# A router's table of overflow places, kept in memory by token instead of by block

## The chip, the cores and the metric

The kernel runs on one core of a Trainium2 chip. The metric is the device time of one execution in microseconds (us); the time of a version is the median of its runs. A profile is one further execution, recorded by the hardware profiler.

## The reference

Two blocks are computed on 256 tokens of width 1024. The first block is a mixer (an RWKV part and a gated linear attention part), an output projection, and a mixture of 32 experts; the second is a two-layer transformer with a context stream of its own. The piece that matters here is the routing of the first block's experts. Cut to that:

```python
gsel = jnp.argmax(coarse, axis=-1)                       # one of 4 groups per token
top_p, top_e = lax.top_k(pf, TOP_K)                      # 2 of the 8 experts of the group
eid = (gsel[:, None] * 8 + top_e).reshape(-1)            # 512 assignments, 2 per token
counts = jnp.bincount(eid, length=32)                    # tokens of each expert
...
ys = (silu(xb @ w_gate[e]) * (xb @ w_up[e])) @ w_down[e] # block by block
out = segment_sum(ys * row_w[:, None], row_tok)          # back to the tokens, weighted
```

## The kernel before, in words

**Two tasks share the engines.** A planner (`_run`) interleaves two streams of work while the program is written: the first block (the function `first`, which ends in `moe`, tiles named with a trailing m), and the conditioning and the context stream of the second block (`second`, tiles named with a trailing c). The order of TensorE's work and of SyncE's loads is the order in which the planner wrote it and is not rearranged later; the other engines are ordered by a scheduler when the program is built.

**Weights come in pieces of 512 KB.** `raw` (line 313) issues each load on SyncE's queue (SP) into one of 13 buffers: 8 called raw, and 5 called room that exist during the context's first feed-forward layers. They are used in rings, so a raw load takes the buffer of the raw load eight before it, and a room load that of the room load five before it. A piece of `wi` or `wo` (feed-forward weights) is split into two parts before TensorE uses it: ScalarE writes `whi` (line 319), VectorE writes `wlo` (line 320), and the buffer is then free; TensorE does 24 matmuls with it (lines 334 to 336, three for each of eight 128x128 tiles). A piece of `moe_gu` (expert weights) is used by TensorE directly, in 4 matmuls (line 1338), and its buffer is free after them.

**Completion counters.** The transfers that SP and ScalarE (ACT) issue share eight completion counters, called DMAHW0 to DMAHW7, which they take in turn. An issue that takes a counter waits until the transfer that had it before has landed.

**The router.** `route` computes for each token its two experts, its rank in each, and from these its place in the blocks of 32 tokens that overflow an expert's first 32. Each expert's first 32 tokens are handled in `moe`, whose first group of four experts follows the router directly. The overflow is handled much later by a loop, `moe_over` (line 1366), which runs `nover` times, a number that the router computes and that can be zero. The loop needs the place of every token in block b: for each of 128 token rows four numbers (two experts by two halves of the tokens). The router builds them in the tile `pos`, [128, 4, 16] (tile name oposm), and writes it to the memory tensor `pos_d`, declared as [16, 128, 4]: block outermost, so that the loop reads one contiguous 2 KB block. Since `pos` has the block innermost and `pos_d` has it outermost, neighbours in `pos` lie 2 KB apart in `pos_d`. Two other transfers go out on ACT's queue near it, `tok_d` (1 MB) and `exp_d` (0.1 KB).

Of the kernel before, what the change touches and what calls it, by code (L numbers as in the profile page):

```python
# [10 lines left out]
F32 = mybir.dt.float32  # L11
# [4 lines left out]
OP = mybir.AluOpType  # L16
# [214 lines left out]
class _Net:  # L231
# [888 lines left out]
    def route(self, ch, x):  # L1120

        nc = self.nc
        mm, V, A = nc.tensor.matmul, nc.vector, nc.scalar
# [4 lines left out]
        b = ch.bank()  # L1128
# [28 lines left out]
        iota = self.c("iota")  # L1157
# [62 lines left out]
        b = ch.bank()  # L1220
# [20 lines left out]
        p = 0  # L1241
        for d in (1, 2, 4, 8, 16):
            V.tensor_copy(inc[1 - p][:, :d], inc[p][:, :d])
            V.tensor_tensor(inc[1 - p][:, d:], inc[p][:, d:], inc[p][:, :32 - d], op=OP.add)
            p = 1 - p
        inc = inc[p]
        V.tensor_tensor(t, inc, nb, op=OP.subtract)
        V.tensor_scalar(t, t, 32.0, -32.0, op0=OP.mult, op1=OP.add)
        pos = ch.tile([128, 4, 16], "opos")
        for a in range(2):  # L1250
            for i in range(2):
                g, r = ch.tile([128, 2], "og", bufs=2), ch.tile([128, 32], "ogt", bufs=2)
                V.tensor_tensor(r, rk[:, i], oh[a][:, i], op=OP.mult)
                V.reduce_sum(g[:, 0:1], r, axis=AX.X)
                V.tensor_tensor(r, t, oh[a][:, i], op=OP.mult)
                V.reduce_sum(g[:, 1:2], r, axis=AX.X)
                V.tensor_tensor(g[:, 1:2], g[:, 1:2], g[:, 0:1], op=OP.add)
                V.tensor_scalar(g[:, 0:1], g[:, 0:1], 32.0, None, op0=OP.is_ge)
                V.scalar_tensor_tensor(g[:, 1:2], g[:, 1:2], 1.0, g[:, 0:1], op0=OP.add, op1=OP.mult)
                V.tensor_scalar(pos[:, 2 * a + i], iota[:, :16], -32.0, -1.0, op0=OP.mult, op1=OP.add)  # L1260
                V.tensor_scalar(pos[:, 2 * a + i], pos[:, 2 * a + i], g[:, 1:2], None, op0=OP.add)
        nc.scalar.dma_start(self.tok_d, self.htok)
        nc.scalar.dma_start(self.pos_d.rearrange("b p a -> p a b"), pos)
        V.tensor_copy(self.cw[:, 0:2], c1)
        V.tensor_copy(self.cw[:, 2:4], c2)
        cmpt = ch.tile([128, 16, 32], "ocm")
# [99 lines left out]
    def moe_over(self, ch_of, x):  # L1366

        nc, tc = self.nc, self.tc
        mm, V, A = nc.tensor.matmul, nc.vector, nc.scalar
        n = nc.values_load(self.nover, min_val=0, max_val=15)  # L1370
        with tc.For_i(0, n, 1) as blk:
            with ExitStack() as es:
                ch = ch_of(es)
                eg = ch.tile([1, 2], "veg", I32)
                nc.sync.dma_start(eg, self.exp_d[bass.ds(blk, 1)])
                ps = ch.tile([128, 4], "vps")
                nc.sync.dma_start(ps, self.pos_d[bass.ds(blk, 1)].rearrange("b p a -> (b p) a"))
                gq = nc.sync.value_load(eg[0:1, 0:1], min_val=0, max_val=7)
                gj = nc.sync.value_load(eg[0:1, 1:2], min_val=0, max_val=3)
                eqs, sw = ch.tile([128, 2, 2, 32], "veq"), ch.tile([128, 2, 32], "vsw")  # L1380
                s = ch.tile([128, 2, 32], "vs")
                htok = ch.tile([128, 2, D], "vtok")
                nc.sync.dma_start(htok, self.tok_d)
                for i in range(2):
                    for a in range(2):
                        V.tensor_scalar(eqs[:, i, a], self.c("iota"), ps[:, 2 * a + i:2 * a + i + 1], None, op0=OP.is_equal)
                    V.tensor_tensor(s[:, i], eqs[:, i, 0], eqs[:, i, 1], op=OP.add)
                    V.tensor_scalar(sw[:, i], eqs[:, i, 0], self.cw[:, i:i + 1], None, op0=OP.mult)
                    V.scalar_tensor_tensor(sw[:, i], eqs[:, i, 1], self.cw[:, 2 + i:3 + i], sw[:, i], op0=OP.mult, op1=OP.add)
                b = ch.bank()  # L1390
                for k in range(KD):
                    for i in range(2):
                        mm(b[:, k * 32:k * 32 + 32], htok[:, i, k * 128:k * 128 + 128], s[:, i],
                           start=(i == 0), stop=(i == 1))
                xt = ch.tile([128, KD, 32], "vx")
                A.copy(xt.rearrange("p a b -> p (a b)"), b[:, :256])
                b = ch.bank()
                for i in range(2):
                    nc.tensor.transpose(b[:32, i * 128:i * 128 + 128], sw[:, i], self.ident)
                swt = ch.tile([32, T], "vwt")  # L1400
                V.tensor_copy(swt, b[:32, :T])
                gu = self.d["moe_gu"].rearrange("(g k m) p (j n) -> g m j p k n", g=8, m=2, j=4)
                dn = self.d["moe_dn"].rearrange("(g k m) p (j n) -> g m j p k n", g=8, m=2, j=4)
                bb = [ch.bank(), ch.bank()]
                for m in range(2):
                    for q in range(2):
                        r = ch.tile([128, 4, 512], "vr", bufs=2)
                        nc.sync.dma_start(r, gu[bass.ds(gq, 1), m, bass.ds(gj, 1), :, q * 4:q * 4 + 4]
                                          .rearrange("g j p k n -> (g j p) k n"))
                        for k in range(4):  # L1410
                            mm(bb[m][:32], xt[:, q * 4 + k], r[:, k], start=(q + k == 0), stop=(q == 1 and k == 3))
                ht = _all(self.swiglu_rows(ch, bb[0], bb[1], 32))
                bb = [ch.bank(), ch.bank()]
                y = ch.tile([32, 2, 512], "vy")
                for m in range(2):
                    r = ch.tile([128, 4, 512], "vr", bufs=2)
                    nc.sync.dma_start(r, dn[bass.ds(gq, 1), m, bass.ds(gj, 1)].rearrange("g j p k n -> (g j p) k n"))
                    for k in range(4):
                        mm(bb[m][:32], ht[:, k], r[:, k], start=(k == 0), stop=(k == 3))
                    A.copy(y[:, m], bb[m][:32])  # L1420
                for d in range(KD):
                    b = ch.bank()
                    mm(b[:, :T], y[:, d // 4, (d % 4) * 128:(d % 4) * 128 + 128], swt, start=True, stop=True)
                    V.tensor_tensor(x[:, d], b[:, :T], x[:, d], op=OP.add)
# [551 lines left out]
def _all(gen):  # L1976

    while True:
        try:
            next(gen)  # L1980
        except StopIteration as e:
            return e.value
# [53 lines left out]
def tile_net(ctx, tc, d, voff, coff, out):  # L2036
    nc = tc.nc
    pool = tc.tile_pool
    net = _Net(tc, d, voff[0], coff[0])
    ctx.enter_context(tc.manual_schedule(engines={mybir.EngineType.PE, mybir.EngineType.SP}))  # L2040
    base = ctx.enter_context(pool(name="base", bufs=1))
    dram = ctx.enter_context(pool(name="dram", bufs=1, space=bass.MemoryType.DRAM))
    net.scr = [dram.tile([2, 16, 4, 32, 32], F32, name=f"scr{i}") for i in range(2)]
    net.pos_d = dram.tile([16, 128, 4], F32, name="pos_d")
    net.exp_d = dram.tile([16, 2], I32, name="exp_d")
    net.tok_d = dram.tile([128, 2, D], F32, name="tok_d")
    names = ("ka", "va", "kb", "vb")
# [89 lines left out]
    with right(name="m2", bufs=1) as sb, ExitStack() as es:  # L2137
        ps = ExitStack()
        ch = _Chain("z", sb, ps.enter_context(pool(name="ps2", bufs=4, space=PSUM)), right, nw_scope=5)
# [36 lines left out]
```

## Time and profile before

| | |
|---|---|
| median of 3 runs | 2956.92 us (2956.76 to 2959.7) |
| the profiled execution's own time | 2956.47 us |
| its span on the core | 2954.7 us |
| TensorE busy | 2829.1 us, 96% of the span |
| mean granted clock of TensorE | 0.978 |
| issue of `pos_d` | at 495.68 us of the span |

The span is the stretch that the profiler sees; the execution's own time is 1.8 us longer. Times in the rows are counted from the start of the span.

### The profile page before, as it was taken

How to read it: one execution, taken by the hardware profiler on the slowest of the kernel's cores; microseconds unless marked ns; L12 is line 12 of the kernel's file. 1: busy time of each engine (PE TensorE's matmuls, PEld its weight loads, DVE VectorE, ACT ScalarE, POOL GpSimd, SP SyncE). 2: the span in 40 equal slices, each digit the busy share in tenths (PEclk: the TensorE clock that was granted, in tenths of full speed). 3: DMA queues.
4: the chain of work that ended last, by engine and by line, in shares of the span. 5: the costliest groups of instructions: out<-in, count | busy, mean ns of one | idle time of the engine just before them, and what ended most of it. 6: DMA issues, size and time to landing. Idle time of an engine off the chain costs nothing. (4 is left out here: it accounts for less than half of the span.)

```text
span 2954.7 us, 55032 instructions
## 1 busy us (share of the span) xinstructions
PE 2829.1 (96%) x22394; PEld 2391.7 (81%) x22394; DVE 1781.4 (60%) x3517; ACT 1235.9 (42%) x2071; POOL 179.2 (6%) x207
## 2 busy tenths in 40 slices
PE   8999787899999999999999899999999999999999
PEld 5656456787756778877887799889999999899999
DVE  4565564454535564555555766767766767666865
ACT  3321123333324443343333444555554545465543
POOL 0110110000000010000000000000200000101100
PEclk9999888999999999999999899999999999999999
DMA  8755856897787888797987555523455555423453
GB/s 320 252 178 173 297 214 167 296 326 265 251 275 275 309 285 326 286 366 302 350 306 286 183 195 184 189 79 116 164 193 194 184 194 197 136 92 138 169 193 131
DMA packets 198897, 667.47 MB, mean 226 GB/s; under 512 B 36850, under 2 KB 37874, under 8 KB 198002
## 3 DMA queue, kind: packets, MB, share of 16 engines
q1 hardware_dynamic: 180144, 656.04, 63.3%
q10 hardware_dynamic: 18498, 7.90, 1.3%
q8 instruction: 176, 2.88, 0.4%
q14 instruction: 79, 0.65, 0.1%
HBM read 658.05 MB, written 5.80 MB: 225 GB/s over the span
## 5 line engine op out<-in xcount | busy, mean ns | idle before, releaser
L320 DVE TENSOR_TENSOR wlo<-raw,whi 128x1024 fp32r<-128x1024 f32 x623 | 769.8, 1236 | 490.5 <-ACT whi L319 476.0
L319 ACT CAST whi<-raw 128x1024 fp32r<-128x1024 f32 x631 | 662.1, 1050 | 770.4 <-issue 274.5
L334 PE MATMUL bz<-hnhz,whi 128*128 128x256 f32 x1920 | 540.6, 282 | 0.7 <-ACT hnhz L328 0.7
L335 PE MATMUL bz<-hnlz,whi 128*128 128x256 f32 x1920 | 533.5, 278 | 4.2 <-DVE hnlz L329 4.2
L336 PE MATMUL bz<-hnhz,wlo 128*128 128x256 f32 x1920 | 532.8, 277 | 0.9 <-DVE wlo L320 0.9
L334 PE MATMUL bc<-hnhc,whi 128*128 128x256 f32 x1504 | 435.1, 289 | 15.5 <-ACT whi L319 14.7
L335 PE MATMUL bc<-hnlc,whi 128*128 128x256 f32 x1504 | 422.2, 281 | 4.5 <-DVE hnlc L469 2.9
L336 PE MATMUL bc<-hnhc,wlo 128*128 128x256 f32 x1504 | 421.9, 280 | 4.4 <-DVE wlo L320 4.4
L334 PEld LDWEIGHTS bz<-hnhz,whi 128*128 128x128 f32 x1920 | 362.1, 189 | 9.6 <-issue 5.7
L335 PEld LDWEIGHTS bz<-hnlz,whi 128*128 128x128 f32 x1920 | 362.2, 189 | 5.6 <-DVE hnlz L329 5.4
L334 PEld LDWEIGHTS bc<-hnhc,whi 128*128 128x128 f32 x1504 | 287.3, 191 | 98.1 <-issue 36.4
L336 PEld LDWEIGHTS bz<-hnhz,wlo 128*128 128x128 f32 x1920 | 362.4, 189 | 1.1 <-DVE wlo L320 1.1
L335 PEld LDWEIGHTS bc<-hnlc,whi 128*128 128x128 f32 x1504 | 287.2, 191 | 6.7 <-DVE hnlc L469 5.2
L336 PEld LDWEIGHTS bc<-hnhc,wlo 128*128 128x128 f32 x1504 | 286.5, 191 | 6.1 <-DVE wlo L320 6.1
L334 PE MATMUL bz<-h0z,whi 128*128 128x256 f32 x704 | 194.3, 276 | 0.0
L335 PE MATMUL bz<-h1z,whi 128*128 128x256 f32 x704 | 194.3, 276 | 0.0
L336 PE MATMUL bz<-h0z,wlo 128*128 128x256 f32 x704 | 194.3, 276 | 0.0
L334 PE MATMUL bc<-h0c,whi 128*128 128x256 f32 x528 | 150.4, 285 | 0.7 <-ACT h0c L328 0.7
L1338 PE MATMUL bm<-raw,mxm 128*32 128x512 f32 x752 | 147.4, 603 | 0.8 <-DMA raw<-moe_gu 0.8
L335 PE MATMUL bc<-h1c,whi 128*128 128x256 f32 x528 | 146.2, 277 | 0.9 <-DVE h1c L329 0.9
L336 PE MATMUL bc<-h0c,wlo 128*128 128x256 f32 x528 | 146.1, 277 | 0.0
L320 DVE TENSOR_TENSOR wlo<-room,whi 128x1024 fp32r<-128x1024 f32 x75 | 91.8, 1225 | 86.0 <-ACT whi L319 81.8
(702 smaller groups left out, 5319.7 us busy)
## 6 DMA issues: line engine op xcount, KB each, us to landing
raw<-wi SPq DMA_DIRECT2D x263, 512.0 KB, 4.6
raw<-moe_gu SPq DMA_DIRECT2D x188, 512.0 KB, 7.2
raw<-wada SPq DMA_DIRECT2D x144, 512.0 KB, 4.9
raw<-wo SPq DMA_DIRECT2D x124, 512.0 KB, 4.5
raw<-wbr SPq DMA_DIRECT2D x108, 512.0 KB, 3.7
raw<-win SPq DMA_DIRECT2D x104, 512.0 KB, 5.2
raw<-moe_dn SPq DMA_DIRECT2D x103, 512.0 KB, 6.0
room<-moe_gu SPq DMA_DIRECT2D x68, 512.0 KB, 9.0
```

The costliest lines, as they stand in the source:

```text
L319: self.nc.scalar.copy(hi, src)
L320: eng.tensor_tensor(lo, src, hi.bitcast(F32), op=OP.subtract)
L334: mm(out, w[0], x[0], start=first, stop=False, **kw)
L335: mm(out, w[0], x[1], start=False, stop=False, **kw)
L336: mm(out, w[1], x[0], start=False, stop=last, **kw)
L1338: mm(b[32 * j:32 * j + 32], xt[:, k, 32 * j:32 * j + 32], r[:, j % 2 * 512:j % 2 * 512 + 512], start=(k == 0), stop=(k == KD - 1))
```

## The change

The table is declared by token: [128, 16, 4] in memory, so that each of the 128 token rows has 64 numbers (256 bytes) in one piece. The tile `pos` has the same shape, [128, 16, 4], so the write of the table copies row to row. VectorE now writes each of the four columns of `pos` with a step of four numbers. The loop reads, for block b, four numbers (16 bytes) out of each token's 256 bytes, 128 pieces 256 bytes apart, where it read 128 pieces of 16 bytes that lay side by side.

```diff
@@ route
-        pos = ch.tile([128, 4, 16], "opos")
+        pos = ch.tile([128, 16, 4], "opos")
...
-                V.tensor_scalar(pos[:, 2 * a + i], iota[:, :16], -32.0, -1.0, op0=OP.mult, op1=OP.add)
-                V.tensor_scalar(pos[:, 2 * a + i], pos[:, 2 * a + i], g[:, 1:2], None, op0=OP.add)
+                V.tensor_scalar(pos[:, :, 2 * a + i], iota[:, :16], -32.0, -1.0, op0=OP.mult, op1=OP.add)
+                V.tensor_scalar(pos[:, :, 2 * a + i], pos[:, :, 2 * a + i], g[:, 1:2], None, op0=OP.add)
         nc.scalar.dma_start(self.tok_d, self.htok)
-        nc.scalar.dma_start(self.pos_d.rearrange("b p a -> p a b"), pos)
+        nc.scalar.dma_start(self.pos_d, pos)
@@ moe_over
-                nc.sync.dma_start(ps, self.pos_d[bass.ds(blk, 1)].rearrange("b p a -> (b p) a"))
+                nc.sync.dma_start(ps, self.pos_d[:, bass.ds(blk, 1)].rearrange("p b a -> p (b a)"))
@@ tile_net
-    net.pos_d = dram.tile([16, 128, 4], F32, name="pos_d")
+    net.pos_d = dram.tile([128, 16, 4], F32, name="pos_d")
```

No engine's instructions change places. On ScalarE the one row that differs is the issue of the table, between the transfer of `exp_d` and the work on the context's feed-forward layer (`wc`, `h0c`, `whi`); this is that piece of the difference, with the counters each row waits for in brackets:

```order
 L1275 DMA exp_d<-oeim 2x16x1 [waits DMAHW2_49,DVE_49]
 L1550 ACTIVATE wc<-bc 128x256 [waits PE_49,Activation_49]
-L1263 DMA pos_d<-oposm 512x16x1 [waits DMAHW4_49,DVE_49]
+L1263 DMA pos_d<-oposm 128x64 [waits DMAHW4_49,DVE_49]
 L328 CAST h0c<-wc 128x256 [waits DVE_49]
 L319 CAST whi<-room 128x1024 [waits DMAHW3_49,Activation_49]
```

The table's write has moved nowhere; it goes from 512 rows of 16 single numbers to 128 rows of 64 numbers. It takes counter DMAHW4 in both.

On SyncE nothing differs. These are its loads around the same place of the program, the same before and after (the number behind a name is the buffer's, which the later text uses to tell pieces apart):

```order
L313 DMA raw_4862<-wi0 128x1024 [waits DMAHW5_49,DMAHW1_49,DVE_49]
L313 DMA raw_4892<-wi0 128x1024 [waits DMAHW6_49,PE_49]
L313 DMA room_4931<-wi0 128x1024 [waits DMAHW7_49,PE_49]
L313 DMA raw_4961<-wi0 128x1024 [waits DMAHW0_49]
L313 DMA room_4999<-moe_gu 128x1024 [waits PE_49]
L313 DMA raw_5004<-wi0 128x1024 [waits DMAHW2_49]
L313 DMA raw_5034<-wi0 128x1024 [waits DMAHW3_49,PE_49]
L313 DMA room_5072<-moe_gu 128x1024 [waits DMAHW4_49,PE_49]
L313 DMA raw_5076<-moe_gu 128x1024 [waits DMAHW5_49]
L313 DMA room_5081<-wi0 128x1024 [waits DMAHW6_49,PE_49]
L313 DMA raw_5111<-wi0 128x1024 [waits DMAHW7_49]
L313 DMA raw_5149<-moe_gu 128x1024 [waits DMAHW0_49,PE_49]
```

The load of `room_5072` waits for counter DMAHW4, the table's, in both versions.

## Rows read from the trace of the kernel before

**Rows 1.** Page, busy time of each engine: us, share, instructions.

```profile
PE 2829.1 (96%) x22394; PEld 2391.7 (81%) x22394; DVE 1781.4 (60%) x3517; ACT 1235.9 (42%) x2071; POOL 179.2 (6%) x207
```

**Rows 2.** Busy time by stretch; columns: stretch, us, each engine, PEclk, DMA share, GB/s.

```profile
553.01:600.00 46.99, 46.99 (x388) 39.27 (x387) 25.11 (x33) 17.22 (x23) 0.00 (x0) 1.00 0.98 377
502.88:553.01 50.13, 31.63 (x205) 26.89 (x205) 14.30 (x18) 11.90 (x17) 0.00 (x0) 0.80 0.87 168
```

**Rows 3.** Waits of TensorE from 490 to 560 us: total, times, longest.

```profile
PE bc L334 <- ACT whi L319: 13.3, 3, 11.0
PE bm L1338 <- DMA room<-moe_gu: 2.7, 1, 2.7
PE bc L336 <- DVE wlo L320: 1.7, 3, 0.8
PE bm L1338 <- DMA raw<-moe_gu: 0.8, 1, 0.8
```

**Rows 4.** Timeline of TensorE, 518 to 543 us: start, length, instruction, [idle before, releaser].

```profile
518.73 0.58 PE L334 MATMUL bc<-hnhc,whi 128*128 128x256 f32 x1 [10.95 <-ACT whi L319]
...
520.58 0.41 PE L335 MATMUL bc<-hnlc,whi 128*128 128x256 f32 x1
520.80 0.41 PE L336 MATMUL bc<-hnhc,wlo 128*128 128x256 f32 x1
...
542.86 1.05 PE L1338 MATMUL bm<-room,mxm 128*32 128x512 f32 x4 [2.71 <-DMA room<-moe_gu]
```

**Rows 5.** Waits of SyncE's queue from 490 to 560 us: total, times, longest.

```profile
SPq L313 <- DMA pos_d<-oposm: 35.1, 1, 35.1
```

**Rows 6.** Timeline of SyncE's issues, 502 to 539 us.

```profile
502.49 1.25 SPq L313 DMA_DIRECT2D raw<-wi  x2
538.93 0.33 SPq L313 DMA_DIRECT2D room<-moe_gu  x1
```

**Rows 7.** The tensor `pos_d`: its issue (duration in ns, start), and time to landing.

```profile
L1263 ACTq DMA_DIRECT2D pos_d<-oposm x1: 742/742/742, 495.7 to 495.7; - x1
...
DMA to landing us min/median/max: 43.2/43.2/43.2
```

**Rows 8.** DMA from 495 to 540 us: queues with packets, MB, share; one issue group.

```profile
q1 hardware_dynamic: 1159, 4.22, 53.9%
q10 hardware_dynamic: 8208, 0.03, 26.6%
...
raw<-wi SPq DMA_DIRECT2D x5, 512.0 KB, 20.9
```

**Rows 9.** DMA over the whole span, issues by kind: KB each, median us to landing.

```profile
raw<-wi SPq DMA_DIRECT2D x263, 512.0 KB, 4.6
...
ttx<-scr ACTq DMA_DIRECT2D x2, 256.0 KB, 10.2
```

**Rows 10.** Timeline of TensorE: 24 matmuls apart; the first group's expert pieces.

```profile
494.50 0.62 PE L1338 MATMUL bm<-room,mxm 128*32 128x512 f32 x2
...
499.79 0.39 PE L334 MATMUL bc<-hnhc,whi 128*128 128x256 f32 x1
...
526.08 0.28 PE L334 MATMUL bc<-hnhc,whi 128*128 128x256 f32 x1
...
528.90 0.28 PE L334 MATMUL bc<-hnhc,whi 128*128 128x256 f32 x1
```

**Rows 11.** VectorE instructions: duration in ns min/median/max, first and last start.

```profile
L1261 DVE TENSOR_SCALAR oposm<-oposm,ogm x4: 216/217/229, 492.6 to 495.4; 128x16 f32<-128x16 f32 x4
L1436 DVE SCALAR_TENSOR_TENSOR silua<-silca,vec x2: 157/160/163, 5.0 to 5.0; 128x8 f32<-128x8 f32 x2
L1437 DVE TENSOR_SCALAR cond<-silua x2: 169/172/175, 5.2 to 5.3; 128x8 f32<-128x8 f32 x2
```

**Rows 12.** Waits of TensorE from 556 us to the end: two on weights.

```profile
PE bc L334 <- ACT whi L319: 1.4, 2, 1.0
...
PE bm L1348 <- DMA raw<-moe_dn: 0.8, 1, 0.8
```

## The prediction

> **What bounds the kernel now.** TensorE is busy 96% of the span [rows 1], so an edit counts only where TensorE stands still or runs slowly. I looked for such a place around the issue of the table, stretch by stretch. From 553.01 to 600 us TensorE is busy without a gap at clock 1.00. In the 50.13 us before that it is busy for only 31.63, at a mean clock of 0.80, and the DMA moves 168 GB/s where it moves 377 right afterwards, although its engines show 87% busy [rows 2]. So 18.50 us of standstill lie in one short stretch, beside slow running. The waits name all of it: 13.3, 2.7, 1.7 and 0.8 us, together 18.5, and every one is for weights: the first and third for a piece that is split before use, the second and fourth for an expert piece [rows 3]. The timeline shows the two large ones, 10.95 us before 518.73 and 2.71 before 542.86. It shows too what comes after the first: neighbouring matmuls start 0.22 us apart [rows 4], the lower of the clock's two levels (1.2 GHz), after eleven idle microseconds.
>
> Next, why the weights are late. SyncE, which issues them, waited once for 35.1 us, and what it waited for is the landing of `pos_d` [rows 5]. In its timeline two issues stand at 502.49, 1.25 us long, and then nothing until 538.93, a load of an expert piece into a room buffer [rows 6]; by the order of the loads that is `room_5072`, the one that takes the table's counter. The table itself was issued at 495.7 and landed 43.2 us later, at 538.9 [rows 7]. In those 45 us the queue of ScalarE carried 8208 packets with 0.03 MB: the table's 8,192 numbers, one packet each. SyncE's queue carried only 4.22 MB, and the five raw loads of `wi` in the stretch took 20.9 us to land [rows 8], against 4.6 us over the whole span [rows 9].
>
> The table thus does harm twice. The loads issued beside it crawl, which gives the wait of 10.95 us; and the loads that should follow are not issued, which gives the waits from 542.86 on.
>
> **The write.** It goes from 8,192 pieces of 4 bytes to 128 pieces of 256 bytes. No row shows a write of 256-byte pieces. From below: at the old price per piece, 43.2 us / 8,192 = 5.3 ns, 128 pieces are 0.7 us. From above: the slowest small transfer on ScalarE's queue, 256 KB, lands in 10.2 us [rows 9]. I take 4.6 us, the landing of a weight piece of sixteen times as many bytes. It then lands at 500.3, before SyncE comes to `room_5072` at 502.49 + 1.25 = 503.7, and the wait of 35.1 us is gone. At 10.2 us it lands at 505.9 and SyncE waits 2.2 us; what covers that is worked out below.
>
> **The loads.** SyncE's next condition is a free buffer. `room_5072` takes the buffer of the room load five before it and `raw_5076` that of the raw load eight before it; both held expert pieces of the first group, which TensorE has used up by 499.79 [rows 10]. The same holds for `room_5081` and `raw_5111`. So these four are issued at once, behind 503.7. After that a load needs one more piece to be split, and TensorE sets that pace.
>
> **TensorE.** At full clock the 24 matmuls of a `wi` piece take 528.90 - 526.08 = 2.82 us, and the first group's twelve expert pieces took 499.79 - 494.50 = 5.29 us, 0.44 each [rows 10]. In the 50.13 us TensorE did 205 matmuls [rows 2]: eight `wi` pieces (192) and three expert pieces (12), within one. With no wait and no slow clock these need 8 x 2.82 + 3 x 0.44 = 23.9 us, say 24.0 with the switches between the two kinds. The stretch shrinks by 50.13 - 24.0 = **26.1 us**: 18.5 of standstill and 7.6 of slow running.
>
> Are the weights there in time? Eleven pieces are 5.8 MB, over 24 us 240 GB/s, well under the 377 that the DMA gives right afterwards [rows 2]. `room_5072` is wanted after seven `wi` pieces, at 502.88 + 7 x 2.82 = 522.6. Were the table to land at 505.9 and the load to take 10.2 us as well, it would be there at about 516.5; the cover is six microseconds, and the table could land some 16 us after its issue before TensorE felt it. What may stay are the short waits for `wlo`, 1.7 us in all [rows 3]; I take nothing, since I put them down to the standstills before them, and keep 1.7 for the range.
>
> **VectorE.** Eight instructions on `pos` write with a step of 16 bytes. The second four take 217 ns each. The nearest row with a step writes 8 numbers 128 bytes apart in 172 ns, beside 160 for a write of as many side by side [rows 11]: 12 ns more for 8 numbers, 25 for 16, 0.2 us for eight instructions; from below nothing. They cost nothing as long as TensorE has its expert pieces to do, until 499.79, and 0.2 us without that cover.
>
> **The loop.** Before and after it would read 128 pieces of 16 bytes. None of its body's instructions stands in the trace: on these inputs no expert overflows and it runs zero times. The new read costs nothing here.
>
> **After 553 us.** What is won there must last to the end. From 556 us on TensorE waited 1.4 us for `whi` at line 334 and 0.8 for an expert piece [rows 12], the kinds that cost 13.3 and 3.5 in the stretch; nothing there is of the size of the gain. The order is fixed, and with buffers fuller than before at the same place of the program no load can come later. All of it stays, and at most these 2.2 us come on top.
>
> **The sum.** The profiled execution took 2956.47 us, 0.45 less than the median of the runs. 2956.47 - 26.1 = 2930.4, which I give as **2930.5**; with 1.7 us of waits kept and 2.2 won on top it runs from 2928 to 2932.5.
>
> **The rivals.** (a) *The splits become the bound.* With the loads in time, each `wi` piece still passes ScalarE and VectorE before TensorE has it. If each of the eight waited as the three for `wlo` did, 1.7 / 3 = 0.57 us [rows 3], 4.5 us would come back: 2935. For it: 13.3 us of the waits name a split. Against it: between the two standstills no wait for a split stands in the rows but those at their ends. (b) *The table lands late all the same*, because what is slow is its way into memory and not the number of its pieces. If the loads beside it run freely but it still lands at 538.9, TensorE works on until 522.6 and then stands until about 542.9, when `room_5072` lands as now. The gain falls by 20.3 us to 5.8: 2951. Against it: 8,192 packets in 43.2 us is a steady cost per packet [rows 7, 8], and weight pieces of 512 KB land in 4.6. (c) *Nothing changes*, the loads being slow for a reason of their own: 2956. Against it the wait that names the table [rows 5]. (d) *Slower, by the step in* `pos`: it decides from 26.1 / 8 = 3.3 us more for each of the eight instructions, on the way to the splits that TensorE waits for; at 4 us each it would be 2956.5 + 32 - 26 = 2962. The row with a step of 128 bytes speaks against it, with 12 ns more, not 3.3 us [rows 11].
>
> The Trainium skill has a rule on rival (d), in "SBUF — State Buffer", section "Door 1: The DMA port swizzle": the memory has lines of 16 bytes, and each access that goes on to a new line pays. With a step of four numbers every write is on a new line. The trace agrees in sign with its 12 ns and not in a size that would matter here.
>
> **How the numbers follow.** The forecast holds with 0.82. Rival (a) has 0.09, (b) 0.04, (c) 0.04, (d) 0.01. The range takes the forecast's 2928 to 2932.5 and rival (a)'s 2935, with a microsecond or two on either side for terms that add: 2926.5 to 2937, which leaves out about one in ten. Faster by over 0.2% (5.9 us, about what a measurement of this kernel can tell from no change) are the forecast, (a) and half of (b): 0.93. Within 0.2% are (c) and the rest of (b): 0.06. Slower: 0.01.
>
> **What would show it.** In the profile of the changed kernel: ScalarE's queue has some 8,000 packets fewer; `pos_d` lands in under 11 us; SyncE's wait for it is gone, with issues going on past 503.7; the `wi` loads beside it land in about 5 us instead of 20.9; TensorE is busy at clock 1.00 from 503 to 527, and what began at 553.01 begins at about 527. I am wrong if `pos_d` still lands after 512; if the standstills go but waits for `whi` and `wlo` take their place in the same stretch; or if the stretch shrinks by 26 us and a later one, above all the loads of the experts' second half, grows.

## The result, and the profile after

| | before | after |
|---|---|---|
| median | 2956.88 us (4 runs, 2956.76 to 2959.7) | 2927.32 us (4 runs, 2924.88 to 2929.02) |
| the profiled execution's own time | 2956.47 | 2927.63 |
| span | 2954.7 | 2925.8 |
| mean granted clock of TensorE | 0.978 | 0.985 |

The ratio is 0.9898, with a 95% interval from 0.9875 to 0.9921, and the medians differ by 29.6 us. The forecast was 2930.5 (2926.5 to 2937), so the time lies within the range. The interval is wide because the changed kernel's runs spread over 4 us, and the experiments below show that this first comparison makes the gain look larger than it is.

The page of the changed kernel, busy times and queues; they answer to [rows 1] and [rows 8]:

```profile
PE 2814.9 (96%) x22394; PEld 2382.0 (81%) x22394; DVE 1781.7 (61%) x3517; ACT 1236.5 (42%) x2071; POOL 179.3 (6%) x207
...
q10 hardware_dynamic: 10434, 7.90, 0.9%
```

Over the whole span ScalarE's queue carries 10,434 packets; before, the profile's page had 18,498 there. The difference is 8,064 = 8,192 - 128: the table goes out in 128 pieces.

The tensor `pos_d` (issue in ns, and time to landing), and the first rows of the waits of SyncE and of TensorE from 490 to 560 us, which answer to [rows 7], [rows 5] and [rows 3]:

```profile
L1263 ACTq DMA_DIRECT2D pos_d<-oposm x1: 352/352/352, 490.0 to 490.0; - x1
...
DMA to landing us min/median/max: 7.8/7.8/7.8
```

```profile
SPq L313 <- PE bm L1338: 33.7, 9, 11.7
SPq L313 <- DVE wlo L320: 14.6, 6, 3.8
```

```profile
PE bc L334 <- ACT whi L319: 1.6, 1, 1.6
PE bc L336 <- DVE wlo L320: 0.8, 1, 0.8
```

SyncE's wait for the table is gone. It now waits for buffers that TensorE and VectorE have yet to free, which costs nothing. Of TensorE's 18.5 us of waits 2.4 are left.

The place in the program that ran from 502.88 to 553.01 us before [rows 2] runs from 497.17 to 524.10 after, with the same 205 matmuls:

```profile
497.17:524.10 26.93, 24.55 (x205) 22.40 (x205) 16.57 (x22) 13.04 (x18) 0.00 (x0) 1.00 1.02 401
```

The stretch shrank from 50.13 to 26.93 us, by 23.2, at clock 1.00 instead of 0.80, and the DMA moves 401 GB/s in it instead of 168. Behind it the two executions take equally long: 2954.7 - 553.01 = 2401.7 and 2925.8 - 524.10 = 2401.7. But the spans differ by 28.9, and the remaining 5.7 us lie ahead of the stretch, which begins at 502.88 in one profile and at 497.17 in the other, although all that the change touches ahead of it is eight small VectorE instructions. A good part of this lead arises in nine microseconds. The time from 170 to 179 us, first in the kernel before, then in the changed one:

```profile
170.00:179.00 9.00, 9.00 (x22) 3.08 (x20) 3.72 (x17) 1.92 (x5) 0.00 (x0) 0.50 0.37 129
```

```profile
170.00:179.00 9.00, 8.21 (x37) 2.70 (x35) 7.05 (x37) 2.70 (x7) 0.00 (x0) 1.00 0.68 204
```

In the profile of before the clock was granted at its lower level (1.2 GHz) for nine microseconds in which TensorE was busy throughout; in the other profile it was not. The first two experiments ask whether that is chance.

### The profile page after: what moved, and what is told of

Same layout as the page of the kernel before. It is cut to its first block, busy times and chain, and to the rows that moved or that the text cites. A ratio compares the mean times of both kernels' runs of the same rounds, so it can differ in the third digit from the quotient of the medians.

```text
span 2925.8 us, 55032 instructions
## 1 busy us (share of the span) xinstructions
PE 2814.9 (96%) x22394; PEld 2382.0 (81%) x22394; DVE 1781.7 (61%) x3517; ACT 1236.5 (42%) x2071; POOL 179.3 (6%) x207
## 3 DMA queue, kind: packets, MB, share of 16 engines
q10 hardware_dynamic: 10434, 7.90, 0.9%
## 5 line engine op out<-in xcount | busy, mean ns | idle before, releaser
L1456 PE MATMUL ba<-raw,cond 128*32 128x512 f32 (+1 forms) x640 | 132.7, 589 | 5.4 <-DMA raw<-wada 5.3
```

The lines of the kernel that those rows point to most:

```text
L1456: nc.tensor.matmul(b[32 * j:32 * j + 32, :nb], self.cond[:, k], r[:, o:o + nb], start=(k == 0), stop=(k == KD - 1))
```

## The experiments

The theory, from the prediction: the scattered write does harm twice, by sharing the DMA engines with the weights and by holding the counter that SyncE's next load wants, and its price is one per piece. The rivals: one of the two harms alone; a price that depends on where the pieces lie. Since the time of a run spreads by several us on the chips of these experiments, the measure is the **stretch**: from the first matmul of the first `wi` piece after the first group's expert pieces to the third place after it with an expert piece (499.79 to 555.83 in the first profile, 56.04 us; after, 494.08 to 526.95, 32.87 us). The first two expectations use a place 2.8 us earlier as its end. The `wi` piece that opens the stretch was there in time in every run; "the first `wi` piece" is the one behind it, and so on from there.

### 1 and 2: both kernels again

No edit.

> The kernel before, unchanged, profiled a second time. In the first pair of profiles the kernel before issues its table at 495.7 us and the changed kernel at 490.0, though nothing ahead of that place differs. If that lead of 5.7 us is chance (a drop of the granted clock near 170 us in one profile), the runs spread by several us and this profile issues the table anywhere from 489 to 497. If it belongs to the change in some way, the issue stands at 495.7 again, within 1 us. The stretch from the first wi piece after the first group's expert pieces (499.8 in the first profile) to the place that stood at 553.0 takes 53.2 us in both theories.

> The changed kernel, unchanged, profiled a second time. Chance theory: its issue of the table lies between 489 and 497 us and its time between 2924 and 2933. Theory that the change itself brings the lead: 490.0 again within 1 us, and 2927.3 within 2 us. In both the same stretch takes 30.0 us, 23.2 less than before.

Measured, on one chip: the kernel before 2950.91 us (12 runs, 2940.91 to 2963.17), the changed one 2932.89 (6 runs, 2925.69 to 2940.57), ratio to the kernel before 0.9943 (0.9922 to 0.9964). The table is issued at 496.7 and at 499.7 us. So the lead is chance: this time the changed kernel is the later one at this place, at 499.7 later than either theory had it. The stretch, however, is 51.66 and 31.49 us, a gain of 20.2. By the place that the expectations use it is about 48.8 and 28.6, where 53.2 and 30.0 were expected: against the first pair the kernel before is 4.4 us shorter and the changed one 1.4. The table of the kernel before landed in 36.9 us here, not 43.2, and the longest wait for `whi` is 8.2 us, not 11.0. The waits of the kernel before, second profile (SyncE's, then TensorE's):

```profile
SPq L313 <- DMA pos_d<-oposm: 29.1, 1, 29.1
```

```profile
PE bc L334 <- ACT whi L319: 10.9, 2, 8.2
PE bc L336 <- DVE wlo L320: 1.7, 3, 0.7
PE bm L1338 <- DMA raw<-moe_gu: 1.2, 1, 1.2
```

### 3: no table

```diff
-        nc.scalar.dma_start(self.pos_d, pos)
+
```

> The table is not written at all (left out: the write; on these inputs nothing reads it). If the write in 128 pieces costs nothing any more, the time is that of the changed kernel within 2 us, and the two short waits for the first wi piece (1.6 and 0.8 us) stay. Rival: pieces of 256 bytes still hold up the loads issued beside them; then these waits go and 2 to 3 us are won over the changed kernel.

Measured: 2928.23 us, 0.9928 (0.9906 to 0.9949). That is 4.7 us under the changed kernel on the same chip (2932.89), more than either theory had, but the two intervals overlap, and the stretch shows none of it: 31.55 us, with waits of 0.40 and 0.75 on the first `wi` piece, against 31.49 with the table. By the stretch, the changed kernel has taken all that the table can give.

### 4 and 12: the small table beside it

```diff
-        nc.scalar.dma_start(self.exp_d.rearrange("b a -> a b")[None], ei[0:1])
+        nc.scalar.dma_start(self.exp_d[None], ei[0:1])
...
-    net.exp_d = dram.tile([16, 2], I32, name="exp_d")
+    net.exp_d = dram.tile([2, 16], I32, name="exp_d")
```

The loop's read of `exp_d` is changed to match.

> The changed kernel with one more edit: the neighbouring small table exp_d goes out as one row of 32 numbers instead of 32 single numbers. Theory: those 32 single pieces are what makes SyncE's issue beside them take 3.8 us and the first wi load land after 7.7 us; then the two short waits (1.6 and 0.8 us) go and the time is 2 to 3 us under the changed kernel. Rival: the slow start has nothing to do with exp_d; the waits stay and the time is that of the changed kernel within 1 us.

> The changed kernel with exp_d as one row, profiled a second time, to see whether its shorter stretch repeats. Theory that exp_d's 32 single pieces hold up the loads: SyncE's two issues beside the table take under 2.5 us together (3.7 to 4.3 in the changed kernel), no wait for whi stands before the second wi piece, and the stretch takes 30.5 to 31.2 us (31.5 to 32.9 in the changed kernel). Rival, chance: 3.7 us or more and a stretch over 31.5. The time itself should be within its spread of the changed kernel's in both.

Measured: stretches of 30.74 and 30.45 us, against 31.49 to 32.87 in three profiles of the changed kernel. SyncE's issues beside the table, first in the second of these runs, then in the third profile of the changed kernel (start, length):

```profile
495.40 1.69 SPq L313 DMA_DIRECT2D raw<-wi  x2
```

```profile
493.00 3.71 SPq L313 DMA_DIRECT2D raw<-wi  x2
```

Two issues take 1.69 us instead of 3.71, and in the second run TensorE has no wait left in the stretch. So 32 single numbers were enough to cost about 2 us of SyncE's time. In the whole, 1 to 2 us are too little to be seen: 2931.49 us (0.9942, 0.9925 to 0.9959), which is 1.4 under the changed kernel on its chip where 2 to 3 were expected, and 2928.78 (0.9924, 0.9911 to 0.9938). It is the version with the shortest stretch, not one whose time is shown to be better.

### 5, 6 and 7: how many pieces, and how close

Run 5 has the tile by token but keeps the memory, and the loop's read of it, by block as in the kernel before, so that four numbers are written at a time; runs 6 and 7 have the memory by token too, leave gaps in it, and their reads match.

```diff
@@ run 5 (pos_d is [16, 128, 4], as before the change)
-        nc.scalar.dma_start(self.pos_d.rearrange("b p a -> p a b"), pos)
+        nc.scalar.dma_start(self.pos_d.rearrange("b p a -> p b a"), pos)
@@ run 6 (pos_d is [128, 16, 8])
-        nc.scalar.dma_start(self.pos_d, pos)
+        nc.scalar.dma_start(self.pos_d.rearrange("p b (h z) -> p (b h) z", z=4)[:, :, 0:2], pos.rearrange("p b (h z) -> p (b h) z", z=2))
@@ run 7 (pos_d is [128, 16, 8])
-        nc.scalar.dma_start(self.pos_d, pos)
+        nc.scalar.dma_start(self.pos_d.rearrange("p b (a z) -> p (b a) z", z=2)[:, :, 0], pos.rearrange("p b a -> p (b a)"))
```

> Memory by block as before, tile by token: the table goes out in 2,048 pieces of 16 bytes. If the cost is one per piece (36.9 to 43.2 us for 8,192), it lands in about 10 us, SyncE is not held, and the stretch from the first wi piece after the first group's expert pieces to the third place with an expert piece (56.0 and 51.7 us before, 32.9 and 31.5 after) takes 31 to 34 us. Rival, that it is the layout in memory (neighbours 2 KB apart) that costs: it lands in over 30 us and the stretch is over 50.

> Memory by token, but with a gap of 8 bytes behind every two numbers: 4,096 pieces of 8 bytes. Per piece: it lands in 18 to 22 us after its issue, SyncE is held for about 10 to 14 us, TensorE's first wait is between 0 and 6 us, and the stretch takes 32 to 40 us. Layout theory: as the changed kernel, under 8 us to landing and a stretch of 31 to 33.

> Memory by token, with a gap of 4 bytes behind every number: 8,192 pieces of 4 bytes as before, but close together, 512 bytes per token. Per piece: it lands in 36 to 44 us and the stretch takes 50 to 57 us, as before the change. Layout theory: it lands in under 15 us and the stretch takes 31 to 35.

Run 5 came out near what the price per piece has: landing in 10.4 us, stretch 33.46, ratio 0.9949 (0.9933 to 0.9966); but SyncE, which was not to be held, was held for 3.3 us. Run 6 missed: 31.5 us to landing where 18 to 22 were expected, SyncE held for 21.6 us, stretch 46.57, 0.9991 (0.9977 to 1.0004). Run 7 missed too, on the far side: it landed in 56.8 us, the stretch took 69.49, and the kernel is slower than before the change: 2967.82 us, 1.007 (1.0049 to 1.0091). Its waits, SyncE's and TensorE's:

```profile
SPq L313 <- DMA pos_d<-oposm: 49.4, 1, 49.4
```

```profile
PE bc L334 <- ACT whi L319: 19.4, 2, 18.9
PE bm L1338 <- DMA room<-moe_gu: 10.6, 1, 10.6
```

So the layout theory is wrong as it stood (pieces close together are not cheap), but one price per piece is wrong too: 4-byte pieces 8 bytes apart cost 56.8 us / 8,192 = 6.9 ns, those of the old layout 4.5 to 5.3. Nor is the landing divided by the count the time of a piece. In run 5 ScalarE's queue has 2,064 packets between 507 and 509 us and none behind them, where the table's issue was at 501.9 and its landing at 512.3: most of its 10.4 us is not spent on pieces. So the agreement of run 5 is partly luck.

### 8: without the counter

```diff
-        nc.scalar.dma_start(self.pos_d.rearrange("b p a -> p a b"), pos)
+        nc.gpsimd.dma_start(self.pos_d.rearrange("b p a -> p a b"), pos)
```

> The kernel before, its 8,192 pieces issued from GpSimd's queue, so that the table no longer takes one of the eight counters that SyncE's loads use. The pieces still share the 16 DMA engines with the loads. Two harms (my theory): SyncE's wait for the table is gone, the standstill before the second wi piece stays at 5 to 11 us, the later ones go, and the stretch takes 38 to 47 us. Rival one, the counter alone does the harm: the first standstill goes too, and the stretch takes 31 to 34. Rival two, the sharing alone does it: 50 to 57.

Measured: 2950.77 us, 1.0009 (0.9996 to 1.0021), stretch 51.21, table landed in 29.1 us. The stretch is the one that rival two had. The waits of SyncE and of TensorE, and what the loads did in the 45 us from 500:

```profile
SPq L313 <- DMA raw<-wi: 25.9, 6, 14.4
```

```profile
PE bc L334 <- ACT whi L319: 12.9, 2, 8.5
```

```profile
q1 hardware_dynamic: 2374, 8.67, 93.7%
```

SyncE no longer waits for the table, and nothing is won. It waits for its own weight loads, up to 14.4 us for one, since those crawl and hold the other counters. The table lands sooner here than from ScalarE's queue (36.9 and 43.2 us), and yet the `wi` loads beside it take 14.1 us in the median (20.9 and 16.2 there). GpSimd's queue also makes up the pieces in another way (144 packets in these 45 us, so many pieces in each), so this is not the kernel before with one thing taken out, and it cannot divide the lost time between the two harms. A free counter, got in this way, did not help.

### 9 and 10: the same count, farther apart

As run 7, with `z=16` (64 bytes apart) and `z=128` (512 bytes apart).

> 8,192 pieces of 4 bytes, memory by token, one number in every 64 bytes. So far such pieces cost 4.5 to 5.3 ns each where neighbours of one token lay 2 KB apart, and 6.9 where they lay 8 bytes apart. Theory: pieces that one after another fall into the same small line of memory wait for each other, and at 64 bytes they no longer do: landing in 36 to 44 us, stretch 50 to 57 us. Rival: any order by token costs 6.9 ns per piece: landing in 54 to 60 us, stretch over 65.

> As the run with a gap of 64 bytes, but one number in every 512 bytes. Both theories as there; if 64 bytes is not far enough and 512 is, this one lands in 36 to 44 us and the other in 54 to 60.

Measured: landings of 27.6 and 24.2 us, stretches of 39.81 and 36.53, ratios 0.9958 (0.9941 to 0.9976) and 0.9953 (0.9934 to 0.9972). Both land sooner than either theory had it, and the stretches are shorter. The waits of run 9, SyncE's and TensorE's:

```profile
SPq L313 <- DMA pos_d<-oposm: 19.6, 1, 19.6
```

```profile
PE bc L334 <- ACT whi L319: 4.3, 1, 4.3
PE bc L336 <- DVE wlo L320: 1.2, 2, 0.8
```

SyncE is held by the table for 19.6 us (15.6 in run 10), and no wait of TensorE follows from that: its only waits stand before the first two `wi` pieces, for loads that were issued before SyncE was held.

### 11: the changed kernel a third time

No edit.

> The changed kernel a third time, for the size of the effect. By the stretch, 20.2 to 23.2 us are won, a ratio to the kernel before of 0.992 to 0.993. If the first comparison's 29.6 us is the size (0.990), this run shows it again; if the 17 us of the second is (0.994), then that. The stretch takes 31 to 33 us in all of them.

Measured: 2930.54 us (2921.45 to 2936.3), ratio 0.9925 (0.99 to 0.995), stretch 31.94. The medians differ by 19.6 us on this chip (17.0 on that of run 2), in line with the stretch's 20.2 to 23.2; the interval is too wide to rule out 0.990 or 0.994. Near 170 us the clock of this profile of the changed kernel stood at the lower level too, so the drop does not belong to the kernel before:

```profile
170.00:179.00 9.00, 9.00 (x22) 3.10 (x20) 3.74 (x16) 2.36 (x6) 0.00 (x0) 0.50 0.35 126
```

The writes of the table from ScalarE's queue together, without runs 4 and 12 (pieces, distance between a token's neighbours in memory, landing, landing divided by the count, SyncE's wait for the table, stretch). Runs 5 to 10 have one profile each, and runs 9 and 10 another chip than runs 5 to 7:

| | pieces | apart | landing us | ns a piece | SyncE's wait | stretch us |
|---|---|---|---|---|---|---|
| before, two profiles | 8,192 of 4 B | 2 KB | 43.2, 36.9 | 5.3, 4.5 | 35.1, 29.1 | 56.04, 51.66 |
| run 7 | 8,192 of 4 B | 8 B | 56.8 | 6.9 | 49.4 | 69.49 |
| run 9 | 8,192 of 4 B | 64 B | 27.6 | 3.4 | 19.6 | 39.81 |
| run 10 | 8,192 of 4 B | 512 B | 24.2 | 3.0 | 15.6 | 36.53 |
| run 6 | 4,096 of 8 B | 16 B | 31.5 | 7.7 | 21.6 | 46.57 |
| run 5 | 2,048 of 16 B | 2 KB | 10.4 | 5.1 | 3.3 | 33.46 |
| after, three profiles | 128 of 256 B | - | 7.8, 6.0, 6.9 | - | none | 32.87, 31.49, 31.94 |
| run 3 | none | - | - | - | none | 31.55 |

## Why the prediction was right, point by point

**The place and the cause** were right. TensorE's wait for weights behind the table's scattered write is gone, together with the drop of the clock that followed it, and leaving the table out altogether (run 3) wins nothing more. All four rivals are out by the first profile after. On (a): the waits that are left stand before the first `wi` piece, and none of the later splits is waited for. On (d): the four instructions that also read `pos` take 230 ns where they took 217 [rows 11] (225 and 226 in the next two profiles), and the four that only write it 168 where they took 162. The estimate for sixteen numbers was 25 ns more, from two rows of different operations; on the same operation it is at most 13. The Trainium skill's rule on 16-byte lines ("SBUF — State Buffer", "Door 1: The DMA port swizzle") thus has its sign again and no size that matters.

**The size** was 26.1 us for the stretch; it is 23.2 in the first pair and 20.2 in the second. TensorE's time of 24.0 us was right within 0.6 (24.55 busy). Two terms were off. The waits that stay were taken as nothing, with 1.7 kept for the range; they are 2.4 in the first profile after and 1.0 in the second. The prediction put them down to the standstills before them; runs 4 and 12 show that part of them comes from `exp_d`, which the change leaves alone. And the price of the scattered write differs between executions, 43.2 and 36.9 us; I had one profile and took its value as fixed. That the median came within 3.2 us of the forecast is partly luck: without the lead ahead of the stretch the profiled time would have been 2927.63 + 5.7 = 2933.3, also in the range. Where both kernels ran again the medians differ by 17.0 and 19.6 us, not by 26.1.

**The landing** of 7.8 us lies between the bounds of 0.7 and 10.2; the 4.6 I took was low. As worked out, it costs nothing. The lower bound left out what does not go with the count of pieces: 128 of them still land in 6.0 to 7.8 us. Of the four loads that were to go out at once behind the table, two did, at 498.13 and 498.92 us; the others followed at 501.27 and 502.59, and no wait of TensorE's came of it. The loads beside the table were forecast at about 5 us and take 10.0 in the median (from 490 to 535 us); SyncE now runs ahead and several are under way at once, which would explain it but was not tested.

**The two harms** are both in the traces. The stop at the counter: from 532 us to the table's landing at 538.9 no packet of any queue moved in the profile of the kernel before:

```profile
DMA packets 0, 0.00 MB, mean 0 GB/s; under 512 B 0, under 2 KB 0, under 8 KB 0
```

SyncE stood at the counter all that time [rows 5], and the piece that TensorE waits for at 542.86 was issued at 538.93 [rows 4, rows 6]. So the waits from there on (2.7 and 0.8 us for expert pieces, 1.5 and 0.5 for the `wi` piece behind them, 5.5 in all) come from the stop, as the prediction had it. In run 7 it is 10.6 us, for a piece issued at 549.97, when the table had landed. Where the table lands sooner the stop is covered: runs 9 and 10 keep SyncE waiting 19.6 and 15.6 us with no later wait of TensorE's. The prediction put that cover at some 16 us after the issue; a landing at 27.6 us was still covered in run 9, where TensorE came to the piece 6.8 us later than in the changed kernel.

The slow loads are the larger harm, 10.95 us in one wait and the slow clock behind it, but not because the table's packets fill the engines while TensorE waits. The queues of SyncE and ScalarE from 505 to 520 us in the kernel before:

```profile
q1 hardware_dynamic: 474, 1.75, 88.4%
q10 hardware_dynamic: 598, 0.00, 6.2%
```

The table's packets took 6.2% of the engines' time, the weights' own 88.4%, which is 0.45 us for each (15 us x 16 engines x 0.884 / 474). From 553 to 600 us they took 0.15 (4,847 packets, 97.8%). What makes a weight packet three times as long beside the table no run shows.

What the theory had wrong is what freeing the counter would win. In run 8 it is free and the waits for expert pieces are gone, as expected, but there are two waits for `whi`, of 4.4 and 8.5 us, and TensorE's waits in the stretch are 14.6 us in all, where they are 13.8 in the second profile of the kernel before. How long the loads behind the table would have taken in the kernel before without the stop stays open, since no run has a late table without slow loads.

**"A steady cost per packet"**, said against rival (b), was wrong: at the same count of pieces, and with the memory by token, the landing goes from 24.2 to 56.8 us as the distance changes. Nor do the packets fill the landing: in the kernel before they had ended by 532 us.

## What to carry to other kernels

Count the pieces of a small transfer, not its bytes: 32 KB in 8,192 pieces slowed the weight loads beside them for some 20 us and held SyncE's queue for 29 to 35, and a transposed layout that is free for the reader moved those pieces to the writer. Look for the engine's wait that names such a transfer, but expect that freeing its counter alone will not help, because the large loads beside it crawl. And where a kernel's runs spread by several us, compare the stretch that the edit touches in several profiles before taking the medians' difference for its worth.

## What was not expected of the hardware

- By the landing divided by the count, 4-byte pieces that a token writes 8 bytes apart cost 6.9 ns each, 64 bytes apart 3.4, 512 bytes apart 3.0, and 2 KB apart 4.5 to 5.3. Pieces of 8 bytes, 16 bytes apart, cost 7.7. That small pieces close together wait for each other would fit but was not shown; why 2 KB is worse again no run tells (its pieces also go out in another order, in which four of them, not written one after another, fill the same 16 bytes).
- The landing can come long after the last packet: in the kernel before no packet moved from 532 to 538.9 us, in its second profile none from 527 to 533.5, in run 7 none from 546 to 549.9, and each time the landing of the table came at the end.
- 32 single numbers from one partition made SyncE's next two issues take 3.7 to 4.3 us in the changed kernel's three profiles, instead of 1.6 to 1.7 in runs 4 and 12.
- The clock of TensorE fell to its lower level for nine microseconds near 170 us, with TensorE busy all through, in the first profile of the kernel before and the third of the changed one, and not in the other three of these two kernels. With whatever else varies there, the table was issued anywhere from 490.0 to 501.9 us in the profiles of all runs.
